# A two-layer trunk: eight blocks of the first feed-forward for both halves of the tokens in seven products of eight

## The chip, the cores and the metric

The kernel runs on one core of a Trainium2 chip. The core has a matrix engine (TensorE, PE in the profile, with its weight loads as PEld), a vector engine (VectorE, DVE), a scalar engine (ScalarE, ACT), GpSimd (POOL) and SyncE (SP, which here issues the DMA transfers). Each engine works through its own queue in order. The metric is the device time of one execution in microseconds, the median of several runs.

## The reference, cut to what matters

Two layers over 1024 tokens of 1024 channels, in float32. Layer 0 is a forgetting attention beside a pooling mixer; layer 1 is RWKV-7 time mixing. After each stands the same feed-forward, of 2816 inner columns:

```
def _swiglu(h, w_gate, w_up, w_down):
    return (jax.nn.silu(h @ w_gate) * (h @ w_up)) @ w_down

# each layer: x = x + mixer(rmsnorm(x)); x = x + swiglu(rmsnorm(x), w_gate, w_up, w_down)
```

The RWKV mixer is a recurrence over the tokens, so half 0 of the tokens must be through it before half 1 can start. The change concerns the feed-forward of layer 0.

## The kernel before, in words

**Numbers.** Every float32 matrix is split into a high part (rounded by a cast on ScalarE) and a low part (the rest, one subtraction on VectorE). A product is three matmuls, high by high, high by low, low by high: `mm3`, lines L163, L164 and L165, each of 128x128 by 128x512. Weights come through `load_part`: a DMA of 256 KB from SyncE into one of two raw buffers (L150, tile "wraw"), the cast (L151, "whi"), the subtraction (L152, "wlo"), with five buffers for the finished parts. Each such piece feeds four blocks, so 12 matmuls.

**Tiling.** The tokens are two halves of 512. The feed-forward's inner columns are 22 blocks of 128. For one half, a block costs 24 matmuls for gate, 24 for up and 24 for down, 72 in all. Per block VectorE multiplies silu(gate) by up (L726 and L732, tile "sg") and splits the result (L260, "h1l"); after each group of four blocks, the down product is added to the residual x (L705) for eight output rows.

**Order of the work.** Attention and out-projection come first (0 to 484 us). Then FFN0 of half 0 alone (`run(ffn(...(0,)...))`, 484 to 843), the RWKV projections of half 0 (`rw.dense`, 843 to 1051), and RWKV's recurrence of half 0 in two jobs of eight heads (1051 to 1501). A job is prepared for four pairs of heads (scans and multiplications on VectorE, small matmuls L1060, evictions L1065 to L1068), then solves a triangular system in 30 dependent steps on VectorE (L1110 and L1112, tile "nu", with transposes L1096, L1099, L1118 and L1120 ahead and behind), then groups of small matmuls (L1130, L1140), then eight chunk steps: matmul z (L1165), copy (L1167), matmul u (L1171), copies on ScalarE (L1173, "uv"), matmuls L1177, L1188 and L1190, state update on VectorE (L1179, L1183, L1184), and on to the next step's z. Closing rows follow (L1208 to L1220).

**The filler.** These chains leave TensorE free, so FFN0 of half 1, a generator called `f1`, is woven into them: at each `yield` of the job `weave` lets `f1` issue as many matmuls as the job asks for, by the table `rw.fr[0]`, one number for each of seven places of the job (its matmuls write tile "fm" and are otherwise L163 to L165). 96 matmuls of `f1` are issued ahead of the projections; what is left of it after the jobs runs on its own (1501 to 1562). Then the projections and the jobs of half 1 follow in the same way, with FFN1 of half 0 as filler and `rw.fr[1]`, and the rest of FFN1 at the end. A scheduler may move an engine's instructions within the order of their priorities.

## Time and profile before

| | |
|---|---|
| median of 3 runs | 2699.88 us (2699.42 to 2700.76) |
| profiled execution, its own time | 2699.79 us |
| its span in the trace | 2698.0 us |
| TensorE busy | 2632.5 us, 98% of the span |
| VectorE busy | 1725.1 us, 64% |
| ScalarE busy | 1298.7 us, 48% |
| granted TensorE clock, mean | 0.996 of full speed |

The profiled execution stands for the runs: its time is 0.09 us below the median, and 1.8 us of it lie outside the span. Busy TensorE time counts matmuls whose ends are modelled and overlap, so what a matmul costs in a full stream is the distance between two starts, not the length of a row.

### The profile page before, as it was taken

The numbers are of one execution on the slowest core, as the hardware profiler recorded it, in microseconds if no ns is written. First come the engines' busy times: TensorE is split into PE (matmuls) and PEld (weight loads), VectorE is DVE, ScalarE is ACT, GpSimd is POOL, SyncE is SP. The second block draws the span as 40 slices with busy tenths as digits, with TensorE's granted clock in tenths as the row PEclk, the third lists the DMA queues.
The fourth block names the chain that finished last, engine by engine and source line by source line (L and its number), as shares of the span: only waits on it lengthen the run. The fifth ranks groups of instructions, "written<-read, shape, count | busy, mean of one in ns | idle before, by whom it ended". The sixth has DMA issues, their size and how long they took to land.

```text
span 2698.0 us, 40269 instructions
## 1 busy us (share of the span) xinstructions
PE 2632.5 (98%) x15368; PEld 2072.6 (77%) x15368; DVE 1725.1 (64%) x2940; ACT 1298.7 (48%) x2297; POOL 49.4 (2%) x139
## 2 busy tenths in 40 slices
...
GB/s 136 58 51 57 42 98 48 83 96 98 96 96 113 172 161 189 129 83 131 148 91 99 195 94 160 168 179 128 87 138 140 92 97 202 101 98 96 97 97 94
DMA packets 170529, 306.11 MB, mean 113 GB/s; under 512 B 18896, under 2 KB 26192, under 8 KB 170336
## 3 DMA queue, kind: packets, MB, share of 16 engines
...
q8 instruction: 120, 1.97, 0.3%
...
## 4 chain that ended last, share of the span: by engine, by line
PE 77%; DVE 14%; ACT 3%; DMA 3%; issue 3%; SPq 0%; DVEq 0%; ACTq 0%
PE mm L163 16%; PE mm L164 16%; PE mm L165 16%; PE fm L163 6%; PE fm L164 5%; PE fm L165 5%; DVE wlo L152 2%; PE mm L175 1%; DVE nu L1112 1%; DVE pd L1110 1%; DVE ZL L1068 1%; DMA wraw<-in_wd_dram 1%; DMA wraw<-in_wu_dram 1%; ACT whi L151 1%; PE o L1177 1%
## 5 line engine op out<-in xcount | busy, mean ns | idle before, releaser
L151 ACT CAST whi<-wraw 128x512 fp32r<-128x512 f32 x738 | 454.0, 617 | 886.8 <-PE mm L164 484.5
L152 DVE TENSOR_TENSOR wlo<-wraw,whi 128x512 fp32r<-128x512 f32 x738 | 501.3, 683 | 446.0 <-ACT whi L151 436.4
L163 PE MATMUL mm<-hh,whi 128*128 128x512 f32 x864 | 343.7, 400 | 6.7 <-ACT hh L355 6.2
L165 PE MATMUL mm<-hh,wlo 128*128 128x512 f32 x864 | 338.7, 392 | 0.0
L164 PE MATMUL mm<-hl,whi 128*128 128x512 f32 x864 | 337.8, 392 | 0.0
L163 PE MATMUL mm<-uh,whi 128*128 128x512 f32 x728 | 283.5, 391 | 0.9 <-DVE x L1318 0.9
L165 PE MATMUL mm<-uh,wlo 128*128 128x512 f32 x728 | 283.1, 389 | 1.2 <-DVE wlo L152 1.2
L164 PE MATMUL mm<-ul,whi 128*128 128x512 f32 x728 | 283.2, 390 | 0.0
L163 PE MATMUL fm<-h1h,whi 128*128 128x512 f32 x528 | 218.7, 415 | 14.8 <-DVE sg L726 10.6
L165 PE MATMUL fm<-h1h,wlo 128*128 128x512 f32 x528 | 208.7, 396 | 0.5 <-DVE wlo L152 0.5
L164 PE MATMUL fm<-h1l,whi 128*128 128x512 f32 x528 | 208.5, 395 | 0.1
L163 PEld LDWEIGHTS mm<-hh,whi 128*128 128x128 f32 x864 | 162.5, 188 | 43.1 <-ACT hh L355 6.9
L165 PEld LDWEIGHTS mm<-hh,wlo 128*128 128x128 f32 x864 | 162.7, 188 | 34.8 <-DVE wlo L152 0.6
L164 PEld LDWEIGHTS mm<-hl,whi 128*128 128x128 f32 x864 | 162.9, 189 | 32.7 <-DVE hl L260 1.3
L163 PE MATMUL fm<-hh,whi 128*128 128x512 f32 x416 | 172.4, 414 | 3.5 <-ACT hh L259 2.8
L164 PE MATMUL fm<-hl,whi 128*128 128x512 f32 x416 | 164.5, 396 | 0.2 <-DVE hl L260 0.2
L165 PE MATMUL fm<-hh,wlo 128*128 128x512 f32 x416 | 164.6, 396 | 0.0
L163 PEld LDWEIGHTS mm<-uh,whi 128*128 128x128 f32 x728 | 136.5, 188 | 34.6 <-issue 2.7
L164 PEld LDWEIGHTS mm<-ul,whi 128*128 128x128 f32 x728 | 136.6, 188 | 31.1 <-issue 1.1
L165 PEld LDWEIGHTS mm<-uh,wlo 128*128 128x128 f32 x728 | 136.7, 188 | 30.0 <-DVE wlo L152 2.0
L705 DVE TENSOR_TENSOR x<-mm,x 128x512 f32<-128x512 f32 x96 | 66.2, 692 | 119.8 <-PE mm L165 119.6
L163 PEld LDWEIGHTS fm<-h1h,whi 128*128 128x128 f32 x528 | 99.5, 189 | 48.7 <-DVE sg L726 13.3
...
## 6 DMA issues: line engine op xcount, KB each, us to landing
wraw<-in_wg_dram SPq DMA_DIRECT2D x176, 256.0 KB, 2.8
wraw<-in_wu_dram SPq DMA_DIRECT2D x176, 256.0 KB, 2.7
wraw<-in_wd_dram SPq DMA_DIRECT2D x176, 256.0 KB, 2.7
wraw<-in_w_in_dram SPq DMA_DIRECT2D x52, 256.0 KB, 2.9
x<-in_xT_dram SPq DMA_DIRECT2D x32, 256.0 KB, 4.8
x<-x SPq DMA_DIRECT2D x32, 256.0 KB, 3.1
wraw<-in_w_k_dram SPq DMA_DIRECT2D x32, 256.0 KB, 2.9
wraw<-in_w_v_dram SPq DMA_DIRECT2D x32, 256.0 KB, 3.0
```

The lines of the kernel that those rows point to most:

```text
L151: k.nc.scalar.copy(hi[0:p, 0:n], raw[0:p, 0:n])
L152: k.nc.vector.tensor_tensor(lo[0:p, 0:n], raw[0:p, 0:n], rd(hi[0:p, 0:n]), ALU.subtract)
L163: nc.tensor.matmul(out, wh, xh, start=(first and i == 0), stop=False)
L164: nc.tensor.matmul(out, wh, xl, start=False, stop=False)
L165: nc.tensor.matmul(out, wl, xh, start=False, stop=(last and i == n - 1))
L175: k.nc.tensor.matmul(out[n * q:n * q + n], w[:, n * j:n * j + n], xs[j], start=c == 0, stop=c + g == len(xs), tile_position=(0, n * q))
L705: nc.vector.tensor_tensor(X[half][m], o, X[half][m], ALU.add)
L1068: nc.vector.tensor_tensor(ZL[h][HS[1 - h], i, bs], s4[HS[1]], self.msk[HS[1]].rearrange("p a t -> p (a t)").unsqueeze(1).broadcast_to([64, ...
L1110: nc.vector.tensor_tensor(pv, nu[:, j + 1:32, j:j + 1].broadcast_to([P, n, j]), nu[:, j:j + 1, 0:j].broadcast_to([P, n, j]), ALU.mult)
L1112: nc.vector.tensor_tensor(nu[:, j + 1:32, 0:j], nu[:, j + 1:32, 0:j], pv, ALU.add)
L1177: nc.tensor.matmul(sp[HS[h], i], BK[h][:, i, c], uv[h][:, i], start=True, stop=True)
```

## The change: what it does

Of the 22 blocks of FFN0, blocks 8 to 15 are taken out of both halves' own loops and computed for both halves together, by a class `Joint`, between block 7 and block 16 of half 0. The gate of two neighbouring blocks for two halves is a product of 2x2 matrices of blocks (halves of tokens, halves of the 1024 channels, two inner blocks). It is computed by a Strassen-Winograd form: seven products of 12 matmuls instead of eight, with sums of the normalized rows (S1 to S4, made once by `rows`, while block 1 to 7's matmuls run) and sums of the weights (t1 to t4, per pair), and sums of the products on the way out. The same is done for up; down stays as it was, with each weight loaded once for both halves. Four pairs make the eight blocks.

For the other 14 blocks half 0 stores each weight's low part to DRAM, and half 1 reads it back by DMA instead of subtracting it on VectorE: 84 stores and 84 reads of 256 KB. Four tiles of half 1's rows (a21) are written to DRAM and read back too. PSUM buffers "mm" go from four to six in these stages, a pool of weights moves in memory, and the first entry of `rw.fr` is changed to the smaller filler: `f1` has 14 blocks, 1008 matmuls, instead of 22, 1584.

```diff
+def load_part(k, ap, p, n, tag="w", w=512, bufs=None, pool=None, key=None):
...
     k.nc.sync.dma_start(dst, ap)
     k.nc.scalar.copy(hi[0:p, 0:n], raw[0:p, 0:n])
+    if key in k.low:
+        k.nc.sync.dma_start(rd(lo[0:p, 0:n]), k.low[key][0:p, 0:n])
+        return hi, lo
     k.nc.vector.tensor_tensor(lo[0:p, 0:n], raw[0:p, 0:n], rd(hi[0:p, 0:n]), ALU.subtract)
+    if key is not None:
+        k.low[key] = k.dram.tile([P, HN], F32, tag="lo" + key, name="lo" + key)
+        k.nc.sync.dma_start(k.low[key][0:p, 0:n], rd(lo[0:p, 0:n]))
     return hi, lo
...
+class Joint:
...
+        for j in range(4):
+            a22 = normed(self.mt("a22"), j + 4)
+            H[1][j + 4] = part(k, pair(k, *M), a22)
+            A["22"].append(H[1][j + 4])
+            yield 0
+            a21 = normed(self.n3("a21"), j)
+            nc.sync.dma_start(keep(j), a21)
+            s1 = self.nt("s1")
+            nc.vector.tensor_tensor(s1, a21, a22, ALU.add)
+            A["S1"].append(part(k, pair(k, *U), s1))
+            yield 0
+            a11 = whole(self.jt("a11", "tt", 3), j)
+            s2 = self.nt("s2")
+            nc.vector.tensor_tensor(s2, s1, a11, ALU.subtract)
+            A["S2"].append(part(k, pair(k, *U), s2))
+            yield 0
+            nc.vector.tensor_tensor(a11, a11, a21, ALU.subtract)
+            A["S3"].append(part(k, pair(k, *M), a11))
+            yield 0
+            a12 = whole(self.jt("a12", "tc", 2), j + 4)
+            nc.vector.tensor_tensor(a12, a12, s2, ALU.subtract)
+            A["S4"].append(part(k, pair(k, *U), a12))
+            yield 0
...
+    def four(self, w, f, out):
+        k, nc, A = self.k, self.k.nc, self.A
+        raw = lambda: k.wp.tile([P, HN], F32, tag="wraw", name=nm(k, "wraw"), bufs=k.rawbufs)
+        b11, b12, b21, b22 = raw(), self.mt("b12"), raw(), self.mt("b22")
+        for t, ap in ((b11, w[f][:, 0:HN]), (b12, w[f + 1][:, 0:HN]), (b22, w[f + 1][:, HN:]), (b21, w[f][:, HN:])):
+            nc.sync.dma_start(t, ap)
+        def product(o, b, a, first=True):
+            yield from mm3(k, o, [(blk(b, j), A[a][j]) for j in range(4)], first, True, True)
+        p11 = self.split(b11)
+        t3, t2, t4 = (self.jt(n, "tt", 3) for n in ("t3", "t2", "t4"))
+        nc.vector.tensor_tensor(t3, b22, b12, ALU.subtract)
+        nc.vector.tensor_tensor(b12, b12, b11, ALU.subtract)
+        nc.vector.tensor_tensor(t2, b22, b12, ALU.subtract)
+        pt2 = self.split(t2)
+        x = pmm(k)
+        yield from product(x, p11, "11")
+        s1 = self.n3("p1")
+        nc.scalar.copy(s1, x)
+        p21 = self.split(b21)
+        nc.vector.tensor_tensor(t4, b21, t2, ALU.subtract)
+        y = pmm(k)
+        yield from product(y, pt2, "S2")
+        u = self.n3("u")
+        nc.vector.tensor_tensor(u, y, s1, ALU.add)
+        pt1 = self.split(b12)
+        yield from product(x, p21, "12", False)
+        out(0, 0, x, None)
+        pt3 = self.split(t3)
+        z = pmm(k)
+        yield from product(z, pt1, "S1")
+        u5 = self.n3("u5")
+        nc.vector.tensor_tensor(u5, z, u, ALU.add)
+        p22 = self.split(b22)
+        v = pmm(k)
+        yield from product(v, pt3, "S3")
+        out(1, 1, v, u5)
+        pt4 = self.split(t4)
+        yield from product(z, p22, "S4", False)
+        out(0, 1, z, u)
+        yield from product(v, pt4, "22", False)
+        out(1, 0, v, u)
...
+    def down(self, f, acts):
+        k, nc = self.k, self.k.nc
+        for m in range(8):
+            if m % 2 == 0:
+                w = [load_part(k, self.ins[f"wd{self.L}"][m:m + 2, :, f:f + 2].rearrange("m p f c -> p m f c"), P, 512)]
+            for half in range(2):
+                o = pmm(k)
+                yield from mm3(k, o, [(blk(w, 2 * (m % 2) + i), acts[half, i]) for i in range(2)])
+                nc.vector.tensor_tensor(self.X[half][m], o, self.X[half][m], ALU.add)
...
+            yield from self.four(self.ins[f"wg{self.L}"], f, gate)
+            yield from behind
+            yield from self.four(self.ins[f"wu{self.L}"], f, up)
+            behind = self.down(f, acts)
+        yield from behind
...
-    k.mm = (k.ps, "mm", 4)
+    k.mm = (k.ps, "mm", 6)
...
-    GP, G0, G1, G2 = ((4,),(),(4,4,4,4,2),(4,4,4,4,2))
-    n = sum(GP) + sum(G0)
-    g0 = ffn(k, ins, 0, (0,), H, X, U, tp, GP)
+    GP, NJ = (4, 4), 4
+    left = NFB - sum(GP) - 2 * NJ
+    G1 = tuple(min(4, left - i) for i in range(0, left, 4))
+    fj, n = sum(GP), sum(GP) + 2 * NJ
+    g0 = ffn(k, ins, 0, (0,), H, X, M, tp, GP, keep=True)
     ahead(g0, 24)
     for m in MO[1][NP:]:
         on[1].add(X[1][m])
-    run(g0)
-    make_h(k, on[1], "ffn0", X[1], M, H[1])
-    run(ffn(k, ins, 0, (0, 1), H, X, U, tp, G0, fb0=sum(GP)))
-    run(ffn(k, ins, 0, (0,), H, X, U, tp, G1, after0, True, n))
+    ahead(g0, 24)
+    jn = Joint(k, ins, 0, X, tp, mp, jp, M)
+    for _ in jn.rows("ffn0", on[1].rstd(), H, U, M, lambda j: rw.dt(f"n{j}")):
+        ahead(g0, 21)
+    run(jn.run(fj, NJ, g0))
+    for j in range(4):
+        t = jn.n3("a21")
+        nc.sync.dma_start(t, rw.dt(f"n{j}"))
+        H[1][j] = part(k, pair(k, *M), t)
+    c_j.close()
+    c_wl, wl = pool("wl", "right")
+    run(ffn(k, ins, 0, (0,), H, X, U, tp, G1, after0, True, n, True))
     rw.ln_exp, rw.mx, rw.wl_bufs, k.sigm = False, U, 2, True
-    f1 = chain(ffn(k, ins, 0, (1,), H, X, M, mp, GP, silu=None), ffn(k, ins, 0, (1,), H, X, M, mp, G2, after0, None, n))
+    f1 = chain(ffn(k, ins, 0, (1,), H, X, M, mp, GP, silu=None, keep=True), ffn(k, ins, 0, (1,), H, X, M, mp, G1, after0, None, n, True))
...
-    rw.fr = [6, 6, 5, 16, 7, 9, 16], [7, 7, 4, 16, 7, 8, 20]
+    rw.fr = [4, 4, 3, 8, 3, 9, 8], [7, 7, 4, 16, 7, 8, 20]
...
```

Line numbers move: the weight's DMA, cast and subtraction are L152, L153 and L157 in the changed kernel, the read of the low part L155, its store L160, the three matmuls of `mm3` L171 to L173, and the lines of the job lie 167 further on (L1110 becomes L1277).

**VectorE in the recurrence of job 0, half 0**, in the order of its instructions. "pd" and "nu" are the dependent steps, "wlo", "sg" and "h1l" rows of the filler. Before:

```order
L1110 TENSOR_TENSOR pd_2417_10430<-nu_2368_10220 128x240
L152 TENSOR_TENSOR wlo_2423_10466<-wraw_2424_10467,whi_2422_10465 128x512
L1112 TENSOR_TENSOR nu_2368_10220<-nu_2368_10220,pd_2417_10430 128x16x15
L726 TENSOR_TENSOR sg_2395_10349<-fm_2389_10309,sg_2395_10349 128x512
L1110 TENSOR_TENSOR pd_2418_10439<-nu_2368_10220 128x240
L152 TENSOR_TENSOR wlo_2426_10472<-wraw_2427_10473,whi_2425_10471 128x512
L1112 TENSOR_TENSOR nu_2368_10220<-nu_2368_10220,pd_2418_10439 128x15x16
L1110 TENSOR_TENSOR pd_2419_10445<-nu_2368_10220 128x238
L1112 TENSOR_TENSOR nu_2368_10220<-nu_2368_10220,pd_2419_10445 128x14x17
L1110 TENSOR_TENSOR pd_2420_10454<-nu_2368_10220 128x234
L732 TENSOR_TENSOR sg_2395_10349<-fm_2402_10366,sg_2395_10349 128x512
L1112 TENSOR_TENSOR nu_2368_10220<-nu_2368_10220,pd_2420_10454 128x13x18
```

and in the changed kernel, where L1277 and L1279 are the two lines of a step:

```order
L715 TENSOR_TENSOR x_1117_4563<-fm_2629_11433,x_1117_4563 128x512
L1277 TENSOR_TENSOR pd_2624_11417<-nu_2593_11280 128x240
L1279 TENSOR_TENSOR nu_2593_11280<-nu_2593_11280,pd_2624_11417 128x16x15
L1277 TENSOR_TENSOR pd_2625_11423<-nu_2593_11280 128x240
L1279 TENSOR_TENSOR nu_2593_11280<-nu_2593_11280,pd_2625_11423 128x15x16
L1277 TENSOR_TENSOR pd_2630_11437<-nu_2593_11280 128x238
L715 TENSOR_TENSOR x_1161_4756<-fm_2637_11465,x_1161_4756 128x512
L1279 TENSOR_TENSOR nu_2593_11280<-nu_2593_11280,pd_2630_11437 128x14x17
L1277 TENSOR_TENSOR pd_2631_11443<-nu_2593_11280 128x234
L1279 TENSOR_TENSOR nu_2593_11280<-nu_2593_11280,pd_2631_11443 128x13x18
```

The subtractions of the weights' low parts are gone from between the steps, and one addition to x stands there (L715, L705 before).

**TensorE in a chunk step of the same job**, from matmul u to the first matmul that reads its copies "uv". Before:

```order
L1171 MATMUL s_2516_11025<-zs_2515_11017,XR_2221_9420 64x64 x8
L163 MATMUL fm_2520_11043<-h1h_2381_10293,whi_2517_11037 128x512
L164 MATMUL fm_2520_11043<-h1l_2382_10294,whi_2517_11037 128x512
L165 MATMUL fm_2520_11043<-h1h_2381_10293,wlo_2518_11038 128x512
L163 MATMUL fm_2520_11043<-h1h_2408_10407,whi_2517_11037 128x512
L164 MATMUL fm_2520_11043<-h1l_2409_10408,whi_2517_11037 128x512
L165 MATMUL fm_2520_11043<-h1h_2408_10407,wlo_2518_11038 128x512
L163 MATMUL fm_2520_11043<-h1h_2434_10518,whi_2517_11037 128x512
L164 MATMUL fm_2520_11043<-h1l_2435_10519,whi_2517_11037 128x512
L165 MATMUL fm_2520_11043<-h1h_2434_10518,wlo_2518_11038 128x512
L1177 MATMUL o_2521_11053<-uv_2512_11004,BK0_2224_9423 64x64
```

and in the changed kernel (L1338 is u, L1344 the reader of "uv"):

```order
L1338 MATMUL s_2726_12033<-zs_2725_12028,XR_2469_10596 64x64 x8
L172 MATMUL fm_2705_11895<-h1l_1322_5404,whi_2702_11889 128x512
L173 MATMUL fm_2705_11895<-h1h_1321_5403,wlo_2703_11890 128x512
L171 MATMUL fm_2705_11895<-h1h_1377_5643,whi_2702_11889 128x512
L1344 MATMUL o_2727_12047<-uv_2722_12015,BK0_2472_10599 64x64
```

Nine filler matmuls have become three.

**SyncE's queue in the jobs of half 0**, weights of the filler. Before, only raw weights:

```order
L150 DMA wraw_2424_10467<-in_wu0_dram 128x512
L150 DMA wraw_2427_10473<-in_wu0_dram 128x512
L150 DMA wraw_2438_10524<-in_wg0_dram 128x512
L150 DMA wraw_2441_10530<-in_wg0_dram 128x512
L150 DMA wraw_2451_10581<-in_wu0_dram 128x512
```

and in the changed kernel, where each raw load is followed by the read of the low part of an earlier one:

```order
L155 DMA wlo_2635_11460<-lo0_d_7_0_5504 128x512
L152 DMA wraw_2647_11499<-in_wu0_dram 128x512
L155 DMA wlo_2643_11492<-lo0_u_4_0_5526 128x512
L152 DMA wraw_2660_11556<-in_wg0_dram 128x512
L155 DMA wlo_2646_11498<-lo0_u_4_512_5534 128x512
L152 DMA wraw_2663_11562<-in_wg0_dram 128x512
L155 DMA wlo_2659_11555<-lo0_g_5_0_5577 128x512
L152 DMA wraw_2673_11706<-in_wu0_dram 128x512
```

Raw loads and reads of low parts now alternate in one queue, and a read of a low part stands ahead of the next raw load.

## Rows read from the trace of the kernel before

**Rows 1.** The page of the profile: the span, the engines (busy us, share of the span, instructions), and from its list of the costliest groups the weight cast on ScalarE (count; busy us, mean ns of one; idle before).

```profile
span 2698.0 us, 40269 instructions
...
PE 2632.5 (98%) x15368; PEld 2072.6 (77%) x15368; DVE 1725.1 (64%) x2940; ACT 1298.7 (48%) x2297; POOL 49.4 (2%) x139
...
L151 ACT CAST whi<-wraw 128x512 fp32r<-128x512 f32 x738 | 454.0, 617 | 886.8 <-PE mm L164 484.5
```

**Rows 2.** Busy time of each engine by stage. Columns: start and end in us, length, then busy us (and instructions) of PE, PEld, DVE, ACT, POOL, the granted TensorE clock, the DMA share and GB/s. In this order: first feed-forward of half 0; then of half 0's job 0 the preparation, the triangular recurrence, the eight-matmul groups behind it, and the chunk loop; of job 1 the preparation with job 0's closing rows, and the recurrence; last, the recurrence of job 0 of half 1.

```profile
484.00:843.00 359.00, 358.12 (x1576) 295.27 (x1575) 169.21 (x259) 127.32 (x207) 0.00 (x0) 1.00 0.33 97
1051.18:1117.60 66.42, 61.93 (x453) 46.81 (x452) 63.56 (x101) 39.02 (x72) 3.70 (x9) 1.00 0.48 155
1117.60:1171.27 53.67, 47.99 (x230) 37.91 (x228) 51.50 (x98) 24.23 (x43) 0.75 (x6) 0.97 0.31 94
1171.27:1191.06 19.79, 19.79 (x321) 15.96 (x320) 11.71 (x18) 8.93 (x15) 0.00 (x0) 0.99 0.29 81
1191.06:1257.56 66.50, 66.50 (x795) 50.79 (x795) 35.21 (x68) 27.53 (x59) 0.00 (x0) 1.00 0.33 104
1266.13:1347.08 80.95, 77.34 (x518) 57.96 (x517) 76.57 (x121) 48.14 (x86) 3.45 (x10) 1.00 0.54 169
1347.08:1398.65 51.57, 47.04 (x225) 37.65 (x223) 49.64 (x97) 19.17 (x35) 0.75 (x6) 0.97 0.28 85
1853.95:1895.62 41.67, 38.79 (x196) 30.89 (x194) 40.07 (x89) 13.96 (x25) 0.75 (x6) 1.00 0.30 89
```

**Rows 3.** Timeline of TensorE in a run of feed-forward matmuls (start us, length us, engine, line, tiles, shape): the first and the last of twelve consecutive rows.

```profile
1173.30 0.39 PE L163 MATMUL fm<-h1h,whi 128*128 128x512 f32 x1
...
1175.80 0.39 PE L165 MATMUL fm<-h1h,wlo 128*128 128x512 f32 x1
```

**Rows 4.** VectorE by line in the recurrence of job 0, half 0 (1117.61 to 1171.26): count | busy us, mean ns | idle before.

```profile
L152 DVE TENSOR_TENSOR wlo<-wraw,whi 128x512 fp32r<-128x512 f32 x18 | 12.2, 684 | 0.6 <-ACT whi L151 0.5
L1118 DVE STREAM_TRANSPOSE XR<-nu 32x1024 f32<-32x1024 f32 x4 | 7.9, 1971 | 0.1
L732 DVE TENSOR_TENSOR sg<-fm,sg 128x512 f32<-128x512 f32 x4 | 2.7, 684 | 0.0
L726 DVE TENSOR_TENSOR sg<-fm,sg 128x512 f32<-128x512 f32 x4 | 2.7, 677 | 0.0
L260 DVE TENSOR_TENSOR h1l<-sg,h1h 128x512 fp32r<-128x512 f32 x3 | 2.1, 689 | 0.0
L705 DVE TENSOR_TENSOR x<-fm,x 128x512 f32<-128x512 f32 x1 | 0.7, 694 | 0.0
```

**Rows 5.** The same view of the preparation of job 0 (1051.18 to 1117.60): the lines of the feed-forward.

```profile
L152 DVE TENSOR_TENSOR wlo<-wraw,whi 128x512 fp32r<-128x512 f32 x12 | 8.1, 686 | 0.3 <-ACT whi L151 0.2
L705 DVE TENSOR_TENSOR x<-fm,x 128x512 f32<-128x512 f32 x8 | 5.5, 691 | 0.2
L260 DVE TENSOR_TENSOR h1l<-sg,h1h 128x512 fp32r<-128x512 f32 x2 | 1.4, 690 | 0.0
L732 DVE TENSOR_TENSOR sg<-fm,sg 128x512 f32<-128x512 f32 x2 | 1.4, 688 | 1.1 <-PE fm L165 1.1
L726 DVE TENSOR_TENSOR sg<-fm,sg 128x512 f32<-128x512 f32 x1 | 0.7, 692 | 0.0
```

**Rows 6.** The same view of the preparation of job 1 (1266.14 to 1347.07): the lines of the feed-forward.

```profile
L152 DVE TENSOR_TENSOR wlo<-wraw,whi 128x512 fp32r<-128x512 f32 x16 | 10.7, 685 | 0.1
L705 DVE TENSOR_TENSOR x<-fm,x 128x512 f32<-128x512 f32 x8 | 5.5, 689 | 0.2
L726 DVE TENSOR_TENSOR sg<-fm,sg 128x512 f32<-128x512 f32 x3 | 2.1, 687 | 0.0
L260 DVE TENSOR_TENSOR h1l<-sg,h1h 128x512 fp32r<-128x512 f32 x2 | 1.4, 690 | 0.7 <-ACT h1h L259 0.7
L732 DVE TENSOR_TENSOR sg<-fm,sg 128x512 f32<-128x512 f32 x2 | 1.4, 688 | 0.0
```

**Rows 7.** Timelines of TensorE, ScalarE and VectorE in one step of the chunk loop of job 0, half 0, put in order of their start (start us, length us).

```profile
1202.07 0.68 PE L1171 MATMUL s<-zs,XR 64*64 64x64 f32 x16
1202.80 0.76 ACT L1173 COPY uv<-s 64x256 f32<-64x256 f32 x2 [0.23 <-PE s L1171]
1205.68 0.42 DVE L1179 TENSOR_TENSOR st<-o,S 128x256 f32<-128x256 f32 x1 [2.22 <-PE o L1177]
1206.03 0.68 PE L1190 MATMUL o<-XR,uv 64*64 64x64 f32 x16
1206.14 0.87 DVE L1183 TENSOR_TENSOR SV<-st,Pc 64x256 f32<-64x256 f32 x2
```

**Rows 8.** DMA issues in the first feed-forward of half 0 (500 to 850): line, queue, count, KB each, median us from issue to landing.

```profile
wraw<-in_wd_dram SPq DMA_DIRECT2D x44, 256.0 KB, 2.7
```

**Rows 9.** The DMA view of the rest of the filler, 1500 to 1560: the total, and the landing of the down weights.

```profile
DMA packets 7242, 12.28 MB, mean 205 GB/s; under 512 B 752, under 2 KB 1776, under 8 KB 7239
wraw<-in_wd_dram SPq DMA_DIRECT2D x4, 256.0 KB, 4.1
```

**Rows 10.** What TensorE waits for in the recurrence of job 0 (1117.61 to 1171.26): us in total, times, longest us.

```profile
PE fm L163 <- DVE sg L726: 5.7, 3, 4.1
```

**Rows 11.** Busy time and clock around the longest of those waits (columns as in rows 2).

```profile
1164.10:1168.10 4.00, 0.25 (x2) 0.00 (x0) 3.97 (x5) 0.00 (x0) 0.00 (x0) 1.00 0.38 120
1168.10:1171.50 3.40, 3.09 (x14) 2.05 (x16) 3.34 (x4) 1.24 (x2) 0.00 (x0) 0.50 0.03 13
```

More of the change, by code (lines that the diff above doesn't have):

```diff
@@ L90, in setup @@
     k.prio, k.cur = {}, 0
+    k.low = {}
     k.cc = k.const.tile([P, NCC], F32, tag="cc", name="cc")
```

73 lines of the change are left out of this document (60 added, 13 removed).

## The prediction

> **What bounds the kernel now.** The page comes first: TensorE is busy in 2632.5 of 2698.0 us [rows 1], so a removed matmul is worth its time wherever nothing else is the limit. The second view is busy time by stage [rows 2]. It shows two kinds of stage. In the feed-forward of half 0 TensorE works 358.12 of 359.00 us and VectorE less than half: matmuls alone count. In the two jobs of half 0 the preparations and recurrences are nearly balanced: in the first preparation TensorE has 61.93 and VectorE 63.56 of 66.42 us, in the first recurrence 47.99 and 51.50 of 53.67, in job 1 77.34 and 76.57 of 80.95, then 47.04 and 49.64 of 51.57. The chunk loop is TensorE's alone, 66.50 of 66.50. So the jobs are stages in which the filler's matmuls fill TensorE exactly as long as VectorE's chain takes, and the filler's own VectorE rows make that chain longer. Third, the lines of VectorE in these stages tell which of its rows belong to the filler [rows 4 to 6].
>
> **The change, term by term.**
>
> *Matmuls.* Eight blocks, gate and up, two halves: 8 x 2 x 2 x 24 = 768 matmuls, which become 4 pairs x 2 x 7 x 12 = 672. In a full stream twelve consecutive rows start 11 steps apart in 1175.80 - 1173.30 = 2.50 us [rows 3], 0.227 us each. 96 x 0.227 = **21.8 us** less, if TensorE stays busy elsewhere.
>
> *Where the matmuls go.* The filler loses 8 x 72 = 576 matmuls. Counted in the order of instructions, the two jobs of half 0 have 1261 filler matmuls before and 715 after, 546 or 123.9 us fewer, and the lone rest of the filler 227 and 197. This work moves into the joint stage, where TensorE needs 264 x 0.227 = 59.9 us for each pair and VectorE, by 60 rows at the 0.68 us of a subtraction of this size [rows 4], 41 us. So it is hidden there as it is now in the feed-forward of half 0, and I add nothing for the sums (0 to 3 us). The question is whether the jobs become shorter by all of the 123.9 us. What they don't give up is a new wait.
>
> *Job 0, preparation and recurrence.* The filler falls by 72 + 49 matmuls, 27.5 us. In the preparation VectorE has 25 filler rows, 8.1 + 5.5 + 1.4 + 1.4 + 0.7 = 17.1 us [rows 5]; 7 are left, since the low parts no longer go over VectorE and fewer blocks pass. 18 rows x 0.68 = 12.3 us leave a VectorE that is busy for 63.56 of 66.42 us; with the 2.9 us in which it idles kept, the stage can't be under 54 us, and I take 57, as some of its idling will come with the shorter cover (TensorE's own need is 66.4 - 72 x 0.227 = 50.1). In the recurrence 30 filler rows, 12.2 + 2.7 + 2.7 + 2.1 + 0.7 = 20.4 us [rows 4], become 8 or 9, which leaves 14.6 us less; two of the four transposes L1118, 1.97 us each [rows 4], go behind the matmuls that wait for them now. 53.7 - (14.6 + 3.9) x 0.95 (its rows overlap a little) is 36, taken 37. The same stage of half 1 takes 41.67 us with TensorE at 38.79 and VectorE at 40.07 [rows 2], so a recurrence with a small filler does run near VectorE's own time. Together -26.1 against -27.5 us: **+1.4**.
>
> *Job 1.* The filler falls by 69 + 62, 29.7 us. Its preparation has 10.7 + 5.5 + 2.1 + 1.4 + 1.4 = 21.1 us of filler on VectorE [rows 6], 12 rows of 0.685 or 8.2 us are left; 80.95 - 12.9 = 68, taken 69.5 (TensorE's need: 65.3). The recurrence goes from 32 filler rows to 8: 51.6 - 24 x 0.685 x 0.95 = 36, taken 37. Together -26.0: **+3.7**.
>
> *Groups and chunk loops.* Behind the recurrence of job 0 the filler falls from 63 to 7 matmuls; the 19.79 us [rows 2] less 12.7 leave 7.1, while two transposes must come ahead, so +1.1. In the chunk loops six to nine matmuls between two dependent ones become three or so. Three take 0.68 us. After matmul u the copies "uv" on ScalarE end 1202.80 + 0.76 = 1203.56, u itself 1202.75 [rows 7], so 0.81 us must be covered: some 0.1 us is bare. After the output matmuls the state update ends 1206.14 + 0.87 = 1207.01, L1190 at 1206.71 [rows 7], 0.3 us with 0 to 5 matmuls to cover it. At 0.2 us for each of eight steps that is +1.5 per loop, **+3**. The new waits are 1.4 + 3.7 + 1.1 + 3 = **9.2 us**. Bounds: nothing, if VectorE's idling shrinks with its load (then every stage is TensorE's again), and 25, if every step of the loops bares the whole 0.81 us (13) and the preparations keep 6 us each beyond TensorE's need.
>
> *Smaller terms.* Building the sums while blocks 1 to 7 run puts up to 21 VectorE rows, 14.1 us, between two blocks whose 48 matmuls take 10.9: +1.5 (0 to 3). The copies in DRAM: a store waits for a subtraction that the next raw load waits for too, and a read of a low part waits for a free buffer with the next raw load behind it. A piece feeds 12 matmuls, so two raw buffers give 2 x 12 x 0.227 = 5.45 us for landing, cast (0.617 [rows 1]) and subtraction (0.68); landing has 4.1, and takes 2.7 [rows 8]. In the rest of the filler 12.28 MB pass now at 205 GB/s, with a landing of 4.1 [rows 9]; 16 more reads make it about 16. If that stage couldn't move more than 256 GB/s it would take 62 us instead of some 54, so 0 to 8, taken +1.5, nearer to the row of 2.7. The clock: +1 (0 to 7, below). Together **+4**.
>
> *The clock by row and rule.* The longest wait of the recurrence, 4.1 us for L726 [rows 10], is followed by 3.40 us at a granted clock of 0.50, 1.2 GHz [rows 11], in which TensorE loses at most 1.7 us. The preparation, with 4.5 us of shorter idling, kept 1.00 [rows 2]. So short waits cost no clock here, and long ones one stretch; one more is the +1.
> The Trainium skill, Perfetto Trace Analysis, section Matmul Optimizations, says that the matrix engine scales its power with its utilization and that matmuls should therefore run back to back in batches. That speaks against a change that thins the stream out; the row agrees for the long wait and not for the short ones. By the rule the thin stages would all lose clock, and the sum would end about 20 us higher than by the row.
>
> **Sum.** 2699.8 - 21.8 + 9.2 + 4 = 2691.2, against the profiled execution's own 2699.79 us, which is 0.1 below the median: **2691 us**. The extras held, the change loses as soon as the new waits pass 17.8 us.
>
> **The rivals.**
> *All of it is kept.* The jobs stay TensorE's, with under 3 us of new waits, and the extras are nothing: 2699.8 - 21.8 + 3 = 2681 (2678 to 2684). For it: the chunk loop has no idling at all now, and fewer foreign rows sit in front of the dependent ones. Against: preparations with VectorE at 96% and nothing left to hide it.
> *The round trips of the chunk loops are bare (the other side).* Each of 2 x 8 steps hands over three times, z to u, u to uv, state to z. If one foreign VectorE or ScalarE row of 0.68 us stands ahead of the copy in two of three, three matmuls no longer cover it: 32 x 0.68 = 22 us on top of 9.2: 2699.8 - 21.8 + 31 + 4 = 2713 (2706 to 2720). From 17.8 us of waits, that is 13 such rows, it decides. For it: now six to nine matmuls stand there, and the table gives the loop less than half. Against: the filler's rows become fewer too.
> *Weights come late.* A landing of 4.6 instead of 2.7 us through the longer queue passes the 4.1 by 0.5 us per two pieces, 0.25 x some 80 pieces = 20 us: 2711. For it: 4.1 at 205 GB/s [rows 9]. Against: the feed-forward stages move 97 GB/s [rows 2], and a store and a read add about as much again at most.
> *The clock falls in the thin stages.* Each wait beyond some 4 us costs a stretch of up to 1.7 us; four stages with three each are 20 us: 2710. Against: only one such stretch follows a recurrence now. This is the case that the rule of the Trainium skill above would make.
>
> **How the numbers follow.** The forecast's own case 0.56 (2684 to 2700), all kept 0.12, bare round trips 0.17, late weights 0.08, clock 0.07. The range **2680 to 2711** takes in the forecast's case, most of the first rival, and the lower half of the others. A measurement of this kernel tells 0.2%, 5.4 us, from no change: under 2694.5 is faster, over 2705.3 slower. Of the forecast's case two thirds lie under 2694.5; with the first rival that is 0.50 and a little of the others, **0.52**. Its upper third, and the lower parts of the others, are **0.27**; the rest is slower, **0.21**.
>
> **What would show it.** Right: the joint stage with TensorE busy throughout at about 60 us a pair; job 0's preparation near 57 us and both recurrences near 37, with VectorE busy all along; job 0's chunk loop at some 47 us (93 matmuls or 21 us less, 1.5 idle); the half-1 stages of the same length as now. Wrong: TensorE waiting for "uv" or "SV" in each step (the second rival), for "whi" or "wlo" with a DMA behind it (the third), or many stretches at 0.50 (the fourth).

## The result and the profile after

The changed kernel takes 2707.7 us (median of 7 runs, 2705.44 to 2710.78) against 2699.42 us: 1.0029 times the time before, 95% interval 1.0018 to 1.0040. It is slower by 8 us, where 2691 us was forecast. Two executions of the experiments below, 4272.7 us in x4 and 4509.3 us in x6, ran at a mean clock of 0.56 and 0.68 and are left out of the ratios and of the lines through runs. The page of the changed kernel, its span and its engines, against [rows 1], and its mean granted clock, 0.996 before:

```profile
span 2703.9 us, 40253 instructions
...
PE 2629.1 (97%) x15272; PEld 2072.9 (77%) x15272; DVE 1744.9 (65%) x2968; ACT 1284.6 (48%) x2281; POOL 46.8 (2%) x139
```

```profile
core 0: 2703.9 us, clock 0.988
```

The span of the profiled execution has grown by 2703.9 - 2698.0 = 5.9 us though 96 matmuls are gone, and the clock has fallen from 0.996 to 0.988 of full speed. At two levels of the clock that is (1 - 0.988) x 2 x 2704 = 65 us at 1.2 GHz instead of 22.

To see where it went, the jobs of half 0 are cut at the same instructions in both kernels. Stages of the kernel before (columns as in rows 2): preparation and recurrence of job 0, its chunk loop with the first closing rows (the groups between the two are in [rows 2]), the other closing rows, preparation and recurrence of job 1, its groups, its chunk loop:

```profile
1053.73:1171.27 117.54, 107.37 (x670) 82.84 (x669) 113.56 (x196) 61.96 (x112) 4.20 (x13) 0.99 0.39 123
1191.06:1267.57 76.51, 76.51 (x847) 56.72 (x846) 39.05 (x74) 33.78 (x70) 1.00 (x2) 1.00 0.32 98
1267.57:1278.21 10.64, 10.64 (x42) 7.35 (x41) 10.08 (x15) 5.06 (x9) 0.32 (x2) 1.00 0.72 222
1278.21:1398.65 120.44, 112.30 (x695) 87.32 (x693) 114.78 (x201) 61.66 (x111) 3.89 (x14) 0.99 0.42 129
1398.65:1419.40 20.75, 20.61 (x323) 16.36 (x322) 15.34 (x20) 8.22 (x14) 0.00 (x0) 1.00 0.32 95
1419.40:1496.58 77.18, 77.18 (x847) 56.57 (x846) 38.57 (x74) 36.78 (x77) 0.00 (x0) 1.00 0.32 98
```

The same of the changed kernel, the groups of job 0 as the second row:

```profile
1167.06:1257.22 90.16, 80.66 (x547) 64.87 (x547) 84.01 (x155) 49.77 (x93) 4.07 (x13) 0.92 0.62 196
1257.22:1264.45 7.23, 6.67 (x263) 5.51 (x263) 7.08 (x6) 2.87 (x5) 0.00 (x0) 1.00 0.21 52
1264.45:1324.55 60.10, 58.47 (x754) 40.87 (x750) 29.00 (x56) 27.69 (x61) 1.02 (x2) 0.97 0.38 114
1324.55:1335.60 11.05, 8.10 (x30) 4.92 (x29) 9.91 (x15) 2.79 (x6) 0.12 (x1) 0.96 0.81 266
1335.60:1432.78 97.18, 87.62 (x575) 67.35 (x576) 86.61 (x159) 52.95 (x97) 3.77 (x15) 0.95 0.60 195
1432.78:1449.82 17.04, 17.04 (x276) 12.62 (x277) 12.49 (x11) 6.15 (x11) 0.00 (x0) 0.53 0.11 34
1449.82:1506.81 56.99, 56.99 (x751) 39.79 (x750) 25.36 (x52) 25.27 (x57) 0.00 (x0) 0.99 0.42 130
```

The fall of the filler explains so much of each stage's fall as its matmuls are worth at 0.227 us [rows 3]; what is left over is what the stage gave back:

| stage of half 0 | filler matmuls | length, us | due, us | given back | forecast |
|---|---|---|---|---|---|
| job 0, preparation and recurrence | 340 to 219 | 117.54 to 90.16 | -27.5 | 0.1 | 1.4 |
| job 0, groups | 63 to 7 | 19.79 to 7.23 | -12.7 | 0.1 | 1.1 |
| job 0, chunk loop | 189 to 93 | 76.51 to 60.10 | -21.8 | 5.4 | 1.5 |
| closing rows, then job 1's preparation and recurrence | 402 to 271 | 131.08 to 108.23 | -29.7 | 6.9 | 3.7 |
| job 1, groups | 66 to 20 | 20.75 to 17.04 | -10.4 | 6.7 | 0 |
| job 1, chunk loop | 189 to 93 | 77.18 to 56.99 | -21.8 | 1.6 | 1.5 |

Together 20.8 us. Ahead of the jobs 4.4 us are given back (113.3 us more for 480 matmuls more, 109.0), behind them 1.4, in half 1's stages 1.1: -21.8 + 4.4 + 20.8 + 1.4 + 1.1 = 5.9.

The largest term beyond its forecast is the group stage of job 1 (6.7 us against 0). Its row above has TensorE busy in all of its 17.04 us and a granted clock of 0.53. Its filler shows the clock in the distance of the starts, the first and the last of six consecutive rows of TensorE's timeline:

```profile
1442.42 0.63 PE L171 MATMUL fm<-h1h,whi 128*128 128x512 f32 x1
...
1444.56 0.63 PE L173 MATMUL fm<-h1h,wlo 128*128 128x512 f32 x1
```

Five steps take 2.14 us, 0.428 each, where it is 0.227 at the full clock. Nothing waits inside this stage, but the fall of the clock begins behind a wait. Just ahead of the stage TensorE waits 3.16 us for the transposed triangle, and 0.93 us after that wait the clock falls. The wait, the time up to the fall and the rest of the stage (columns as in rows 2):

```profile
1429.62:1432.78 3.16, 0.00 (x1) 0.00 (x1) 3.06 (x6) 0.63 (x2) 0.00 (x0) 1.00 0.55 166
1432.78:1433.71 0.93, 0.93 (x58) 0.93 (x60) 0.93 (x1) 0.00 (x0) 0.00 (x0) 1.00 0.00 0
1433.71:1449.82 16.11, 16.11 (x230) 11.69 (x223) 11.56 (x11) 6.15 (x11) 0.00 (x0) 0.50 0.12 36
```

In [rows 11] a fall that follows a wait lasts 3.40 us; this one lasts 17.1 us, 1.0 of them in the chunk loop. From the start of job 0 to the end of job 1's loop the changed kernel's trace has 44.4 us at 0.50 in seven stretches, and each begins in a wait of 1.5 to 3.2 us or at most 1.1 us behind one. Before, it was 6.8 us in two stretches. What TensorE waits for from job 0's chunk loop to job 1's (us in total, times, longest):

```profile
PE s L1227 <- DVE ZL L1235: 4.4, 2, 3.0
PE t L1196 <- ACT kn L1192: 3.4, 2, 3.0
PE s L1297 <- DVE t L1287: 3.2, 1, 3.2
PE s L1338 <- DVE zs L1334: 1.6, 1, 1.6
```

### The profile page after: what moved, and what is told of

It reads as the page before. It is cut to its first block, busy times and chain, and to the rows that moved or that the text cites. A ratio compares the mean times of both kernels' runs of the same rounds, so it can differ in the third digit from the quotient of the medians.

```text
span 2703.9 us, 40253 instructions
## 1 busy us (share of the span) xinstructions
PE 2629.1 (97%) x15272; PEld 2072.9 (77%) x15272; DVE 1744.9 (65%) x2968; ACT 1284.6 (48%) x2281; POOL 46.8 (2%) x139
## 4 chain that ended last, share of the span: by engine, by line
PE 78%; DVE 13%; DMA 4%; ACT 3%; issue 2%; SPq 0%; DVEq 0%; ACTq 0%
PE mm L171 17%; PE mm L172 17%; PE mm L173 17%; PE fm L171 5%; PE fm L173 5%; PE fm L172 5%; DVE wlo L157 1%; DVE pd L1277 1%; DVE nu L1279 1%; PE mm L183 1%; DVE ZL L1235 1%; PE s L1332 1%; PE o L1344 1%; PE s L1338 1%; PE o L1357 1%
## 5 line engine op out<-in xcount | busy, mean ns | idle before, releaser
L153 ACT CAST whi<-wraw 128x512 fp32r<-128x512 f32 x658 | 404.4, 616 | 760.3 <-PE mm L172 390.5
L157 DVE TENSOR_TENSOR wlo<-wraw,whi 128x512 fp32r<-128x512 f32 x574 | 389.3, 682 | 355.4 <-ACT whi L153 326.4
L171 PE MATMUL mm<-hh,whi 128*128 128x512 f32 x864 | 343.6, 400 | 6.9 <-ACT hh L363 6.1
L173 PE MATMUL mm<-hh,wlo 128*128 128x512 f32 x864 | 338.7, 392 | 0.0
L171 PE MATMUL mm<-uh,whi 128*128 128x512 f32 x632 | 246.0, 391 | 0.9 <-DVE x L1485 0.9
L172 PE MATMUL mm<-ul,whi 128*128 128x512 f32 x632 | 245.7, 390 | 0.0
L173 PE MATMUL mm<-uh,wlo 128*128 128x512 f32 x632 | 245.5, 389 | 0.0
L171 PEld LDWEIGHTS mm<-hh,whi 128*128 128x128 f32 x864 | 162.4, 188 | 42.9 <-ACT hh L363 6.9
L173 PEld LDWEIGHTS mm<-hh,wlo 128*128 128x128 f32 x864 | 162.5, 188 | 35.0 <-DVE wlo L157 0.6
L171 PE MATMUL fm<-hh,whi 128*128 128x512 f32 x416 | 172.7, 415 | 3.6 <-ACT hh L267 2.8
L173 PE MATMUL fm<-hh,wlo 128*128 128x512 f32 x416 | 164.9, 396 | 0.0
L171 PE MATMUL fm<-h1h,whi 128*128 128x512 f32 x336 | 143.7, 429 | 5.2 <-DVE x L715 2.8
L171 PEld LDWEIGHTS mm<-uh,whi 128*128 128x128 f32 x632 | 118.5, 188 | 30.3 <-issue 4.8
L173 PE MATMUL fm<-h1h,wlo 128*128 128x512 f32 x336 | 138.5, 412 | 0.0
L172 PE MATMUL fm<-h1l,whi 128*128 128x512 f32 x336 | 137.5, 409 | 0.0
L173 PEld LDWEIGHTS mm<-uh,wlo 128*128 128x128 f32 x632 | 118.6, 188 | 24.4
L715 DVE TENSOR_TENSOR x<-mm,x 128x512 f32<-128x512 f32 x80 | 55.1, 691 | 82.5 <-PE mm L173 82.0
L171 PEld LDWEIGHTS fm<-hh,whi 128*128 128x128 f32 x416 | 79.1, 190 | 30.1 <-issue 7.8
```

The source lines that it names most:

```text
L153: k.nc.scalar.copy(hi[0:p, 0:n], raw[0:p, 0:n])
L157: k.nc.vector.tensor_tensor(lo[0:p, 0:n], raw[0:p, 0:n], rd(hi[0:p, 0:n]), ALU.subtract)
L171: nc.tensor.matmul(out, wh, xh, start=(first and i == 0), stop=False, skip_group_check=again)
L172: nc.tensor.matmul(out, wh, xl, start=False, stop=False, skip_group_check=again)
L173: nc.tensor.matmul(out, wl, xh, start=False, stop=(last and i == n - 1), skip_group_check=again)
L715: nc.vector.tensor_tensor(X[half][m], o, X[half][m], ALU.add)
```

## The experiments

Three theories. **Clock**: thin filler lowers TensorE's clock, and that costs time where nothing waits. **Waits**: what is lost is bare waits for VectorE and ScalarE. **Late weights**: the copies in DRAM delay the filler's pieces. "Given back" is meant as in the table. Ratios are to the kernel before on the same chip, with their 95% intervals.

### The kernel before with thin groups (x4)

```diff
-    rw.fr = [6, 6, 5, 16, 7, 9, 16], [7, 7, 4, 16, 7, 8, 20]
+    rw.fr = [6, 6, 5, 5, 7, 9, 16], [7, 7, 4, 16, 7, 8, 20]
```

> The kernel before with one number of its filler table changed: the place behind the recurrence asks for 5 filler matmuls a time instead of 16, so 18 and 24 stand in the group stages of half 0's jobs instead of 63 and 66; the 90 left over run in the lone rest. No joint product, no copies in DRAM, the same matmuls in all. Clock theory (the changed kernel loses because TensorE's clock falls where the filler is thin): half-clock time appears in or behind the group stages, 10 to 17 us in all beside the 6.8 us that are there before, and the kernel loses 4 to 8 us. Wait theory (it loses by bare waits for VectorE and ScalarE alone): 1 to 3 us of waits per group stage, no more half-clock time than before, 2 to 4 us slower.

Measured: 1.0017 (1.0006 to 1.0027), 4.6 us. The two group stages:

```profile
1170.74:1187.79 17.05, 16.78 (x275) 12.48 (x275) 7.54 (x12) 5.31 (x9) 0.00 (x0) 0.50 0.21 63
1394.64:1413.01 18.37, 12.62 (x281) 9.86 (x281) 14.08 (x16) 4.87 (x9) 0.00 (x0) 0.81 0.19 59
```

In job 0 TensorE is busy for 16.78 of 17.05 us, at 1.2 GHz throughout; 45 filler matmuls fewer should have taken 10.2 us off 19.79, and 7.5 of it come back, with 0.3 us of waits. This is the clock, by one number of the table and without any part of the change. Here too the fall begins behind a wait ahead of the stage, of 3.47 us, and 0.85 us after its end:

```profile
1165.11:1168.58 3.47, 0.00 (x1) 0.00 (x1) 3.41 (x5) 0.00 (x0) 0.00 (x0) 1.00 0.26 76
1168.58:1169.43 0.85, 0.85 (x4) 0.72 (x5) 0.85 (x1) 0.54 (x1) 0.00 (x0) 1.00 0.00 0
```

The kernel before has that wait as well, 4.1 us long [rows 10], and is at 0.50 for 3.4 us behind it; with the thin stage it is 20.5 us. In job 1 the same edit gave back 7.2 us in another way: TensorE idles 5.75 of 18.37 us, a wait of 5.8 us for the filler's L726, and the clock is low behind it. So job 0's stage shows the clock theory for the length of the fall, though a wait opens it; job 1's shows mostly a wait.

### The change with fuller groups (x2)

```diff
-    rw.fr = [4, 4, 3, 8, 3, 9, 8], ...
+    rw.fr = [4, 4, 3, 16, 3, 9, 8], ...
```

> The changed kernel with that number back from 8 to 16: 40 and 44 filler matmuls in the two group stages instead of 7 and 20, taken from the lone rest. Clock theory: the 17 us at 1.2 GHz behind job 1's recurrence go, the group stage of job 1 is 6 us cheaper after its extra matmuls are counted, and the kernel gains 5 to 8 us (2699 to 2703). Wait theory: only the waits ahead of the groups are covered, some 2 us gained. Late-weights theory: nothing gained, since the pieces come no sooner.

Measured: 0.9989 (0.9978 to 0.9999), so 0.4% or some 11 us better than the change, more than any theory had. The group stages with 40 and 44 filler matmuls:

```profile
1258.01:1276.79 18.78, 18.78 (x296) 14.67 (x296) 13.85 (x13) 5.84 (x10) 0.00 (x0) 0.73 0.23 73
1437.90:1456.36 18.46, 18.46 (x301) 14.21 (x301) 14.36 (x14) 7.36 (x13) 0.00 (x0) 0.83 0.32 91
```

The clock is 0.73 and 0.83 in them. Job 1's stage gives back 2.7 instead of 6.7 us, job 0's 4.2 instead of 0.1, but the chunk loop behind it only 0.9 instead of 5.4 and job 1's preparation 0.3 instead of 3.8. The lone rest, which lost 65 matmuls, gives back 4.9 instead of 1.4. The sum over the jobs is 9.7 instead of 20.8 us.

### Useless matmuls in the changed kernel (x3)

(`junk` is a copy that ScalarE makes for it, in lines left out here.)

```diff
...
             gps = pst(k, "s", k.sbufs)
+            for _ in range((12 if b == 0 else 6) if half == 0 else 0):
+                nc.tensor.matmul(gps, k.bones, junk, start=True, stop=True)
...
             xps = pst(k, "s", k.sbufs)
+            for _ in range(6 if half == 0 else 0):
+                nc.tensor.matmul(xps, k.bones, junk, start=True, stop=True)
```

> The changed kernel with 30 useless matmuls of 128x128 by 128x512 in each group stage of half 0 (12 ahead of the first group, 6 ahead of each other one; their results are overwritten), 60 x 0.227 = 13.6 us of work that nothing needs, and one ScalarE copy for their input. Clock theory: they keep the clock up, the group stage of job 1 stays at 2.4 GHz, and the kernel's time changes by less than 4 us either way, since 5 to 9 us come back by the clock and 4 to 5 fall into waits. Wait theory: only what falls into waits is free, so it is 8 to 10 us slower.

Measured: 1.0038 (1.0026 to 1.0050), 0.1% or 2 to 3 us above the change's own ratio, for 13.6 us of useless work. Job 1's first 59 us and its group stage:

```profile
1337.36:1396.50 59.14, 54.06 (x354) 40.88 (x355) 48.05 (x76) 33.05 (x60) 1.13 (x7) 0.83 0.56 177
1439.35:1457.35 18.00, 18.00 (x304) 14.05 (x305) 12.69 (x11) 6.58 (x12) 0.00 (x0) 0.91 0.19 60
```

The stage without the 12 useless matmuls ahead of it is 18.00 us long at a clock of 0.91, with 18 useless and 10 more filler matmuls in it, where it was 17.04 at 0.53. A wait of 2.6 us stands ahead of it here too, and the fall behind that lasts 3.4 us. But job 1's preparation, which was not touched, ran at 0.83 in this execution (0.92 in the same stretch of the change's). The total fits the clock theory; it doesn't separate it from chance in the preparation.

### A still fuller table (x8)

```diff
+    rw.fr = [4, 4, 3, 16, 4, 9, 12], ...
```

> The changed kernel with a fuller filler table, [4, 4, 3, 16, 4, 9, 12]: 832 filler matmuls in the jobs of half 0 instead of 715, 40 to 48 in the group stages and 93 instead of 69 in the chunk loops, 117 fewer in the lone rest. Clock theory: the jobs lose next to nothing to the clock, some 10 us gained (about 2697). Wait theory: the covered waits give 3 to 5 us. If the rest needs its filler to cover the loads of the next stage, 3 to 5 us of that are given back there.

Measured: 1.0023 (1.0014 to 1.0032), worse than the kernel with one number changed. The jobs give back 10.6 us, like x2's, but the rest, down to 80 matmuls, gives back 12.4. There TensorE waits for a low part of the next stage's weights (us in total, times, longest):

```profile
PE mm L173 <- DVE wlo L157: 7.7, 1, 7.7
```

So the forecasts of 2697 and of 3 to 5 us were both too good. Filler is not free to move: the rest covers the loads of the next stage.

### Low parts on VectorE again (x5)

```diff
-    g0 = ffn(k, ins, 0, (0,), H, X, M, tp, GP, keep=True)
+    g0 = ffn(k, ins, 0, (0,), H, X, M, tp, GP)
(the same in the two other calls)
```

> The changed kernel without the copies of low parts in DRAM: half 1 subtracts them on VectorE again (84 subtractions more, 84 stores and 84 reads fewer), joint product and filler table as in the change. Clock theory and wait theory alike: about 55 of the 84 subtractions fall into the jobs of half 0, 37 us more for VectorE, of which the preparations and recurrences, where VectorE sets the pace, take some 25: the kernel is 10 to 25 us slower than the changed one (2718 to 2733). Late-weights theory (the copies themselves delay the pieces): it is faster by 2 to 8 us, and the stage ahead of the jobs is 2 to 3 us shorter.

Measured: 1.0053 (1.0041 to 1.0065), 0.24% or 6.5 us above the change's ratio. Preparation and recurrence of both jobs take 101.50 and 100.57 us where the change has 90.16 and 97.18, with VectorE busy for 96 and 97% of them:

```profile
1167.53:1269.03 101.50, 88.71 (x591) 70.11 (x590) 97.72 (x180) 54.62 (x100) 4.04 (x13) 0.97 0.42 128
1350.71:1451.28 100.57, 90.04 (x589) 70.77 (x589) 97.24 (x179) 55.36 (x100) 4.20 (x15) 0.96 0.43 132
```

The copies help, by less than the 10 to 25 us that the clock and wait theories had, and the stage ahead of the jobs is no shorter without them (4.4 us given back, as in the change). The late-weights theory falls here. In the changed kernel's rest the down weights and low parts do land late, by the DMA view of 1507 to 1565 (median us to landing last):

```profile
DMA packets 8423, 14.43 MB, mean 249 GB/s; under 512 B 885, under 2 KB 1909, under 8 KB 8419
wraw<-in_wd_dram SPq DMA_DIRECT2D x4, 256.0 KB, 4.6
wlo<-lo_d SPq DMA_DIRECT2D x4, 256.0 KB, 4.9
```

but TensorE waits 0.5 us there for a cast weight.

### The copies alone (x6)

The kernel before with `load_part`'s keys and `keep=True` as in the diff, nothing joint.

> The kernel before with the copies of low parts in DRAM alone (132 stores and 132 reads), all else as before, filler table too. By the sum's own terms: VectorE loses some 80 subtractions or 55 us in the jobs of half 0, so the idle 10.2 and 8.1 us of TensorE in the two preparations with their recurrences shrink to some 6 and 5, and the kernel gains 5 to 9 us. Late-weights theory: the queue's reads come late and it loses 5 to 15 us, by waits for a low part. Clock theory says nothing on it but that half-clock time doesn't grow.

Measured: 1.0019 (1.0010 to 1.0028), slower, though its profiled execution, at 2698.25 us the fastest of its runs, has a span 2.1 us under that of before. In that one job 0's preparation and recurrence are 5.1 us shorter with the same filler, at the clock of 1.00:

```profile
1056.71:1169.16 112.45, 104.29 (x668) 82.16 (x668) 97.82 (x166) 61.48 (x112) 3.78 (x13) 1.00 0.61 200
```

which is the forecast's VectorE term. Job 1's give 5.7 us, and its groups take 7.6 back: the scheduler put 114 instead of 66 filler matmuls there, behind waits for the filler's multiplication, 6.2 us the longest (us in total, times, longest, both jobs):

```profile
PE fm L171 <- DVE sg L736: 10.6, 4, 6.2
```

The stage ahead of the jobs, in which the stores are, is 3.0 us longer. What the median loses beside this one execution stays open.

### Six blocks, and half 1's norm later (x7, x9)

```diff
-    GP, NJ = (4, 4), 4
+    GP, NJ = (4, 4), 3
+    rw.fr = [4, 4, 3, 16, 4, 9, 12], ...
(x9 beside it)
-    ahead(g0, 24)
+    ahead(g0, 60)
...
-        ahead(g0, 21)
+        ahead(g0, 20)
```

> The changed kernel with six joint blocks instead of eight (16.3 us of matmuls saved instead of 21.8), and the fuller table [4, 4, 3, 16, 4, 9, 12]: 835 filler matmuls in the jobs of half 0 and 221 in the lone rest behind them. Clock theory: group stages with 42 and 48 filler matmuls and a rest as long as before lose 8 to 10 us in all, so 2694 to 2698, faster than the kernel before. Wait theory (chains that are bare because filler is missing anywhere): as the changed kernel with its matmuls back, 2703 to 2708.

> The same with half 1's norm finished later: 60 instead of 24 matmuls of half 0 are issued between the squares of its rows and the sum over them, which in the changed kernel TensorE waits 2.67 us for at 506.6 us. If that wait is only a matter of place, 2 to 3 us are gained against the kernel with six blocks; if VectorE is what is short there, the wait moves and nothing is gained.

Measured: 0.9993 (0.9984 to 1.0001) and 0.9997 (0.9986 to 1.0008). The first, at 2698.80 us, is just above the 2694 to 2698 of the clock theory and below the 2703 to 2708 of the other; from the kernel before it can't be told apart. The second gained nothing: TensorE's wait for the sums of squares, 2.7 us at its longest in the change,

```profile
PE mm L315 <- DVE sq L310: 3.8, 2, 2.7
```

became 0.3 us, and a wait for ScalarE's cast of half 0's activations took its place:

```profile
PE mm L171 <- ACT h1h L267: 3.9, 2, 3.4
PE mm L315 <- DVE sq L310: 0.3, 1, 0.3
```

### Four blocks, and six with full groups (y1, y2)

```diff
+    GP, NJ = (4, 4), 2
+    rw.fr = [5, 5, 4, 16, 5, 9, 12], ...
(y2)
+    GP, NJ = (4, 4), 3
+    rw.fr = [4, 4, 3, 24, 3, 9, 12], ...
```

> The changed kernel with four joint blocks instead of eight (10.9 us of matmuls saved) and the table [5, 5, 4, 16, 5, 9, 12]: 1018 filler matmuls in the jobs of half 0, 63 and 66 of them in the group stages as in the kernel before, 182 in the lone rest. Clock theory: no half-clock time in the group stages and half as much as in the changed kernel in the preparations, waits and clock together lose 3 to 6 us in the jobs and 3 to 4 ahead of them, so 2 to 5 us faster than the kernel before. Wait theory (what is lost goes with the filler missing anywhere, half of it is missing here): half the loss of the changed kernel against half the saving, 3 to 5 us slower than before.

> The changed kernel with six joint blocks and the table [4, 4, 3, 24, 3, 9, 12]: 75 and 80 filler matmuls in the group stages, 69 in each chunk loop, 201 in the lone rest. Clock theory: the 6 to 9 us at 1.2 GHz in each group stage of the kernel with 42 and 48 there are gone, some 5 us gained against it (about 0.9975 of the kernel before). Wait theory: nothing gained by moving 65 filler matmuls from the loops and the rest into a stage that has no waits.

Measured: 0.9997 (0.9985 to 1.0009) and 0.9987 (0.9978 to 0.9996). The first is between the theories. The second has the lowest ratio of all, 2698.87 us against 2701.41, with 75 and 80 filler matmuls in its group stages:

```profile
1226.52:1250.78 24.26, 24.26 (x331) 18.98 (x331) 15.89 (x16) 10.18 (x17) 0.00 (x0) 0.93 0.39 119
1415.19:1440.50 25.31, 24.63 (x337) 19.43 (x336) 16.05 (x17) 7.80 (x13) 0.00 (x0) 0.98 0.40 128
```

They run at 0.93 and 0.98 and give back 1.8 and 1.4 us, where x7 with 42 and 48 gave back 2.9 and 3.4 at 0.83 and 0.77. The group stages so give back some 3 us less than x7's, but the whole gains 1.6 us and not the 5 of the clock theory, and that is within the intervals: this pair doesn't tell the theories apart.

### Useless matmuls in the kernel before with thin groups (y3), and x4 again

```diff
...
+            for _ in range(11 if half == 0 else 0):
+                nc.tensor.matmul(gps, k.bones, junk, start=True, stop=True)
(and as many ahead of xps; the table's number is 5 as in x4)
```

> The kernel before with its groups' number at 5, as in the first experiment, and 44 useless matmuls of 128x128 by 128x512 in each group stage of half 0 in place of the 45 and 42 filler matmuls that went to the rest (11 ahead of each group; their results are overwritten): 88 x 0.227 = 20.0 us of work that nothing needs. In that first experiment the group stage of job 0 ran 17.0 of its 17.05 us at 1.2 GHz with 0.3 us of waits. Clock theory: the group stages are back at 2.4 GHz and some 20 us long as in the kernel before, so each hides 7 of its 10 us of useless work, and the kernel is only 4 to 9 us slower than with the number at 5 alone. Wait theory (the clock follows the waits and costs nothing by itself): all 20 us come on top.

> The kernel before with its groups' number at 5 once more, on the chip of the run with the useless matmuls, to be set beside it: 4 to 5 us slower than the kernel before as in its first run.

Measured: 1.0088 (1.0075 to 1.0102) and 1.0022 (1.0010 to 1.0033), 2726.45 and 2707.70 us. 18.8 of the 20 us came on top, as the wait theory had it in the sum. By stages it is both. Job 0's groups with the useless matmuls, and without them in x4 again:

```profile
1173.44:1193.44 20.00, 20.00 (x319) 15.63 (x318) 5.25 (x9) 4.91 (x9) 0.00 (x0) 0.99 0.13 40
```

```profile
1170.49:1186.17 15.68, 15.09 (x276) 11.43 (x275) 7.41 (x12) 5.28 (x9) 0.00 (x0) 0.58 0.23 69
```

4.3 us longer for 10.0 us of work, at 0.99 instead of 0.58: within the stage the clock gives back the rest. The time at 0.50 behind the wait for L726 is 3.41 us with the useless matmuls and 13.66 without, although that wait is the longer one with them, 4.8 us against 3.5:

```profile
1170.30:1173.71 3.41, 2.99 (x7) 2.42 (x8) 2.73 (x5) 0.62 (x1) 0.00 (x0) 0.50 0.38 109
```

```profile
1169.93:1183.59 13.66, 13.06 (x209) 9.73 (x207) 7.47 (x11) 4.72 (x8) 0.00 (x0) 0.50 0.26 78
```

The longer wait is part of 2.8 us by which the preparation and recurrence grew, so job 0 as a whole is 7.1 us longer up to its chunk loop, and 2.9 of the 10.0 us are free. In job 1 the time at half clock stays as it was, 6.8 us. It begins in the wait of 5.8 us for L726, which the useless matmuls didn't shorten, and all of the work comes on top. My expectation had put both stages down to the clock.

## Why the prediction was wrong, point by point

**The matmuls and the joint stage** were right. A pair of the joint stage and the two recurrences of the jobs in the changed kernel:

```profile
668.80:728.60 59.80, 59.80 (x266) 49.51 (x265) 38.82 (x62) 16.90 (x29) 0.00 (x0) 1.00 0.18 53
1220.00:1257.22 37.22, 33.79 (x157) 27.13 (x153) 34.09 (x77) 12.95 (x23) 1.60 (x7) 0.95 0.55 168
1396.00:1432.78 36.78, 32.62 (x183) 25.91 (x181) 34.77 (x78) 16.72 (x30) 1.69 (x7) 1.00 0.57 179
```

59.8 us for a pair with TensorE busy throughout and VectorE at 38.8, where 59.9 and 41 were forecast; 37.2 and 36.8 us for the recurrences, where it was 37 for both. Job 0's preparation, from its first scan at 1164.50 to 1220.00, took 55.5 us, where it was 57.

**The waits in the jobs** were of the forecast's order, and below it. TensorE's idle time from the start of job 0 to the end of job 1 grows from 18.4 to 24.2 us, by 5.8 (differences of length and busy time in the two tables of stages), where 9.2 were forecast. They are in other places: not in each step of the chunk loops, whose later steps have no waits, but at their first step (zs, 1.6 us), ahead of the groups (3.2), and in job 1's preparation at its first norm (kn, 3.0) and at a small matmul that waits for VectorE's ZL (3.0).

**The clock** is the step that failed: "+1 (0 to 7)". The jobs give back 20.8 us, of which 5.8 are waits. Of the other 15, the group stage of job 1 has 6.7, at half speed and without a wait inside it. In the other stages the clock can have cost at most half of the time at 0.50, which comes to some 5 us: 2.5 in the closing rows and job 1's preparation, 1.7 and 0.5 in the chunk loops. Some 3 us of the two chunk loops are neither wait nor clock; that they come from filler in more and smaller pieces is not shown. So the term is 6.7 us at the least and some 11 at the most, where it was 1.

The step read [rows 11] as "short waits cost no clock here, and long ones one stretch", with 3.4 us to a stretch, and added one stretch. The runs showed more stretches behind shorter waits, and a far longer one. The seven falls in the jobs begin at waits of 1.5 to 3.2 us, all shorter than the 4.1 us of that row. Behind the last of them, with 20 filler matmuls left in the group stage, the clock stayed at 0.50 for 17.1 us. The kernel before shows the same by one number of the table (x4), and useless matmuls bring it back to 3.4 us (y3). The group stage of job 0 had 0.99 with 63 filler matmuls [rows 2], and the prediction put nothing on the clock there when it took 56 of them away.

The rival on the clock, at 0.07 and 2710 us, came nearest to the 2707.7 measured, and partly by luck. It had twelve stretches of at most 1.7 us each behind waits beyond 4 us; the runs have seven behind shorter waits, and the 4.4 us ahead of the jobs help to make up the same sum.

The rule that the prediction weighed and left (the Trainium skill, Perfetto Trace Analysis, section Matmul Optimizations: the matrix engine scales its power with its utilization, so matmuls should run back to back) agrees with this stage: 0.53 behind a wait of 3.16 us, with TensorE's rows busy all along and 32x32 matmuls for most of them.

How much time the clock is worth can also be read between executions of one kernel, which run the same instructions. In y1's 12 runs the fastest is 2693.14 us at a mean clock of 0.993, the slowest 2709.74 at 0.988. A line through the runs of one kernel, time against half-clock time, has a slope of 0.29 to 0.47 us per us in the nine sets of ten or more runs of the experiments, and of 0.23 to 0.44 in the four sets of the kernel before beside them. At these slopes the 65 - 22 = 43 us more of the changed kernel are worth 10 to 20 us. The changed kernel's own seven runs, which lie within 5.3 us, have a slope of 0.13 only. This is a relation between runs; that waits and clock move together in it is not excluded.

**Early rows** were forecast at 1.5 us (0 to 3); the stage ahead of the jobs gave back 4.4, 2.7 of it in one wait for the sum of squares. **The copies in DRAM**: 1.5 was forecast for them, and the rest gave back 1.4, of which 0.5 is a wait for a cast weight. No run shows a limit of 256 GB/s, from which the bound of 8 us came: that stage moved 249 GB/s on average and up to 403 in one of its slices, with landings of 4.6 to 4.9 us. So the agreement of 1.5 and 1.4 is luck. **Bare round trips in every chunk step**, the rival for the other side, didn't come: job 1's loop gave back 1.6 us, the forecast's number.

What stays open is how the 15 us divide in the stages that have waits as well. There a lower clock can cost nothing: job 0's preparation and recurrence had 13.7 us at 0.50 and gave back 0.1.
